# Two decoder layers on one core: both norm roots ahead of the first silu, one explicit silu table load a layer, the fourth mixer group's root from a pair of matmuls, and another list of order shifts

## The chip, the cores and the metric

The kernel runs on one core of a Trainium2 chip. The metric is the device time of one execution in microseconds (us), taken as the median of several runs. Before the change that is 2046.87 us (three runs, 2046.76 to 2048.48). One execution was also recorded by the hardware profiler; its own time is 2045.58 us, and the span from its first to its last instruction is 2043.8 us.

Five queues work side by side: PE (the matrix engine, TensorE), DVE (VectorE), ACT (ScalarE), POOL (GpSimd) and SP (SyncE, which here only issues DMAs). Each works through its own list in order. An instruction waits on semaphores for what other engines must have finished, and everything behind it in the same list waits with it.

## The reference

A decoder trunk of two layers on 1024 tokens of width 1024, in float32.

```python
for l in range(DEPTH):
    h = rmsnorm(x, attn_norm[l])
    proj = h @ w_in[l]
    ...
    y_a = mla_attention(...)          # latent attention, rotary key
    y_b = short_gated_conv(...)
    y_c = multiscale_pool(...)
    y_d = swa_sink_attention(...)     # sliding window, sinks
    groups = jnp.stack([y_a, y_b, y_c, y_d], axis=2)
    gf = gf * lax.rsqrt(jnp.mean(gf * gf, axis=-1, keepdims=True) + RMS_EPS)
    x = x + mixed @ w_o[l]
    h2 = rmsnorm(x, ffn_norm[l])
    gate, up = jnp.split(h2 @ w_gate_up[l], 2, axis=-1)
    x = x + (jax.nn.silu(gate) * up) @ w_down[l]
return rmsnorm(x, final_norm)
```

Each of the four mixer groups has its own RMSNorm (256 channels), and so has the input of the feed-forward part (1024 channels). "Root" below means the reciprocal square root of such a norm.

## The kernel before

**Layout.** Activations are held with channels on the 128 partitions and tokens along the free axis, in two halves of 512 tokens (`HALVES = (1, 0)`, so the second half of the tokens comes first). A float32 product is made of three matmuls of a reduced type (fp32r): each operand is split into a high part (`CAST` on ACT, L280) and a low remainder (`TENSOR_TENSOR` subtract on DVE, L283), and `mm3` (L260) adds high x high, high x low and low x high. Nearly all PE work is L260.

**A root.** `SumSq` squares the channel tiles on ACT (L324) and adds them on DVE (L326, L332). `rnorm` then sums over the partitions with a matmul against a matrix of ones and makes the root on ACT and DVE:

```python
if t in self.hl:                       # the sum was split into a pair
    for i, h in enumerate(self.hl.pop(t)):
        pe.matmul(p, ones_r, R.ap(h), start=i == 0, stop=i == 1)     # L340
else:
    pe.matmul(p, ones, a, start=True, stop=final is None)            # L343, plain float32
act.activation(r0, p, AF.Ln, scale=1.0 / n)                          # L349
act.activation(r0, r0, AF.Exp, scale=-0.5)                           # L350
act.activation(q, r0, AF.Square)                                     # L351
dve.scalar_tensor_tensor(...)                                        # L352, last reader of p
dve.scalar_tensor_tensor(...)                                        # L355
```

`SumSq(n, pair)` decides between the two forms: with `pair` the finished sum is split by ACT and DVE (`half_split`, one CAST and one subtract of 128x512) and the sum over partitions is two fp32r matmuls (L340). Without it the sum goes to PE as one float32 matmul, which the profile records as two (L343). `group_scale(g)` uses the pair for group b, and `norm_a` for group a; groups c and d use the float32 form. Each group has one root per token half and layer.

**The join of the two parts of a layer.** When the last group is ready, `out_last` finishes the output projection of one token half, adds it to the residual and splits the result for the feed-forward products. After the two halves come, in program order: the plain gate and up products of block f = 0 for the first half (`plain(0)`), that half's root, the silu of the gate (`plain_gates`: multiply by the root into a buffer of the ring "tp", then `silu`, which is ACT L1453 and a POOL multiply L1454), `combine(0)`, the product with up (`plain_acts`), the first products of blocks 1 and 2 (`early`), `combine(1)`, the second half's root, `plain(1)`, `combine(2)`, the second half's silu, `combine(3)`. `combine(j)` makes the sums and differences of the two halves that the seven-product scheme of the feed-forward part needs (ACT L1142, L1143; DVE L1132, L1145, L1151, L1153), each split into high and low. Its four results come from the ring "tp" too, which has three buffers.

**Tables.** ACT evaluates Ln and Exp with one loaded table and Silu with another. A load is an instruction of its own (`ACT_TABLE_LOAD`). One is written out at the start (L140, for Ln and Exp); the others are put in by the compiler in front of the function that needs them and carry that function's line.

**Order.** The program is traced once in Python order. Then a planner (class `Order`) lists each engine's instructions by estimated costs, PSUM banks are handed out from that plan, and a table of numbers, `MOVES`, shifts single instructions or short blocks in each engine's list: `e,i,n,d` takes n instructions at place i of engine e and puts them d places later (earlier if negative). The engines are numbered PE 0, ACT 1, DVE 2, POOL 3, SP 4. The final order is forced on the program; waits follow from the data, the buffers and the banks.

Of the kernel before, what the change touches and what calls it, by code (L numbers as in the profile page):

```python
# [18 lines left out]
P = 128  # L19
# [92 lines left out]
def trunk_kernel(ctx: ExitStack, tc: tile.TileContext, ins, out, given=None):  # L112
# [185 lines left out]
    class SumSq:  # L298
# [35 lines left out]
        def rnorm(self, t, cols=whole, tag="t", final=None):  # L334
# [15 lines left out]
            act.activation(r0, r0, AF.Exp, scale=-0.5)  # L350
# [67 lines left out]
    for l in range(L):  # L418
# [254 lines left out]
        def group_scale(g):  # L673

            sg = SumSq(2 * P, g in "b")
            for t in range(2):
                for c in range(2):
                    sg.add(t, F.ap(y[g][c][t]))
                r = sg.rnorm(t)
                for c in range(2):  # L680
                    a = F.ap(y[g][c][t])
                    mul_to(a, a, F.ap(r))
                F.free(r)
# [747 lines left out]
        def plain_gates():  # L1431
            for f, u, pg, pu in waiting:
                gate = tmp("tp")
                mul_to(gate, pg, r2[u])
                silu(gate, r2[u])
                gates.append((f, u, gate, pu))
            waiting.clear()

        def plain_acts():
            for f, u, gate, pu in gates:  # L1440
                acts[f][u] = F.half()
                mul_to(F.ap(acts[f][u]), pu, gate)
            gates.clear()
# [7 lines left out]
        def silu(g, r):  # L1451
            nonlocal last_silu
            last_silu = act.activation(g, g, AF.Silu)  # L1453
            pool.tensor_tensor(out=g, in0=g, in1=r, op=ALU.mult)  # L1454
# [123 lines left out]
        plain_acts()  # L1578
# [4 lines left out]
        r2.append(F.ap(ss2.rnorm(HALVES[1], tag="pv")))  # L1583
        plain(1)
# [692 lines left out]
```

## Time and profile before

| what | value |
|---|---|
| median of three runs | 2046.87 us (2046.76 to 2048.48) |
| the profiled execution | 2045.58 us, span 2043.8 us |
| mean granted PE clock | 0.998 of full speed |
| DMA moved | 302.37 MB, mean 148 GB/s |
| table loads on ACT | 11, of which 5 in each layer and 1 at the start |

How to read it: the page gives busy time per engine and the chain of work that ended last. Two more views are used. The list of waits names, for an engine, who released it and how long it sat idle. The timeline lists instructions in order of time, equal neighbours merged: start, length of the merged stretch, engine, line, operation, tiles, count, and in brackets the idle time just before it and what ended it. Matmuls overlap at their ends, so the distance between starts says more than the lengths. Layer 0 runs from the start to about 1004 us and layer 1 from there; the joins described above lie at 371 to 440 us and 1380 to 1445 us.

### The profile page before, as it was taken

How to read it: one execution, taken by the hardware profiler on the slowest of the kernel's cores; microseconds unless marked ns; L12 is line 12 of the kernel's file. 1: busy time of each engine (PE TensorE's matmuls, PEld its weight loads, DVE VectorE, ACT ScalarE, POOL GpSimd, SP SyncE). 2: the span in 40 equal slices, each digit the busy share in tenths (PEclk: the TensorE clock that was granted, in tenths of full speed). 3: DMA queues.
4: the chain of work that ended last, by engine and by line, in shares of the span. 5: the costliest groups of instructions: out<-in, count | busy, mean ns of one | idle time of the engine just before them, and what ended most of it. 6: DMA issues, size and time to landing. Idle time of an engine off the chain costs nothing.

```text
span 2043.8 us, 26551 instructions
## 1 busy us (share of the span) xinstructions
PE 2025.6 (99%) x9422; PEld 1677.5 (82%) x9422; DVE 1511.1 (74%) x2443; ACT 994.4 (49%) x1743; POOL 551.7 (27%) x420
## 2 busy tenths in 40 slices
PE   9999999999999999999999999999999999999998
PEld 7887888878888888888888888888788888888887
DVE  8789979987666578555657898899876666675555
ACT  7447657753333335444433676668433333354342
POOL 0100000037777772000002000000578667710000
PEclk9999999999999999999999999999999999999999
DMA  5211223335555557766413112242455555487642
GB/s 180 99 67 43 79 84 103 133 125 189 171 186 169 181 183 241 267 208 211 144 45 118 37 42 92 63 150 95 148 183 178 185 173 172 159 304 245 205 165 96
DMA packets 142119, 302.37 MB, mean 148 GB/s; under 512 B 13857, under 2 KB 60961, under 8 KB 141985
## 3 DMA queue, kind: packets, MB, share of 16 engines
q1 hardware_dynamic: 141984, 300.66, 43.9%
q8 instruction: 74, 1.21, 0.2%
q14 instruction: 61, 0.49, 0.1%
HBM read 212.00 MB, written 87.56 MB: 147 GB/s over the span
## 4 chain that ended last, share of the span: by engine, by line
PE 94%; DVE 3%; ACT 1%; issue 1%; DMA 0%; POOL 0%; SPq 0%; DVEq 0%; ACTq 0%
PE ps_mm L260 37%; PE ps_s L260 29%; PE ps_t L260 11%; PE ps_pv L260 8%; PE ps_pv L1044 2%; PE ps_t L1032 1%; PE ps_s L978 1%; PE ps_s L980 1%; PE ps_s L979 1%; PE ps_s L573 1%; PE ps_s L850 1%; PE ps_pv L634 1%; PE ps_t L622 1%; PE ps_t L343 1%; DVE u L286 0%
## 5 line engine op out<-in xcount | busy, mean ns | idle before, releaser
L260 PE MATMUL ps_mm<-u,u 128*128 128x512 f32 (+1 forms) x3378 | 833.3, 391 | 5.2 <-ACT u L280 4.0
L260 PEld LDWEIGHTS ps_mm<-u,u 128*128 128x128 f32 x3378 | 616.8, 188 | 131.6 <-ACT u L280 4.8
L260 PE MATMUL ps_s<-u,u 128*128 128x512 f32 x2670 | 634.4, 389 | 1.6 <-DVE tn L352 1.0
L260 PEld LDWEIGHTS ps_s<-u,u 128*128 128x128 f32 x2670 | 500.6, 188 | 108.2 <-DVE tn L352 1.5
L283 DVE TENSOR_TENSOR u<-u,u 128x1024 fp32r<-128x1024 f32 (+2 forms) x400 | 448.2, 1141 | 175.9 <-ACT u L280 137.8
L280 ACT CAST u<-u 128x1024 fp32r<-128x1024 f32 (+2 forms) x400 | 344.9, 881 | 395.4 <-PE ps_s L260 62.7
L260 PE MATMUL ps_t<-u,u 128*128 128x512 f32 (+1 forms) x1124 | 254.6, 377 | 0.4 <-DVE tn L352 0.4
L260 PEld LDWEIGHTS ps_t<-u,u 128*128 128x128 f32 x1124 | 202.3, 188 | 40.3 <-DVE tn L352 0.8
L1454 POOL TENSOR_TENSOR tp<-tp,u 128x512 f32<-128x512 f32 x80 | 127.6, 1595 | 342.2 <-ACT tp L1453 342.2
L260 PE MATMUL ps_pv<-u,u 128*128 128x512 f32 x744 | 177.4, 389 | 0.0
L260 PEld LDWEIGHTS ps_pv<-u,u 128*128 128x128 f32 x744 | 139.6, 188 | 29.0
L1453 ACT ACTIVATE tp<-tp 128x512 f32<-128x512 f32 x80 | 50.6, 633 | 214.5 <-DVE tp L359 214.3
L1041 POOL MEMSET u<- 128x128 f32 x32 | 6.2, 221 | 467.8 <-PE ps_mm L260 117.1
L749 POOL TENSOR_TENSOR u<-u,u 128x512 f32<-128x512 f32 x4 | 5.4, 1342 | 382.0 <-PE ps_t L622 289.9
L280 ACT CAST u<-ps_t 128x512 fp32r<-128x512 f32 (+3 forms) x132 | 65.2, 503 | 49.9 <-PE ps_t L1032 25.6
L285 ACT ACTIVATE u<-u,par 128x512 fp32r<-128x512 f32 x100 | 70.4, 717 | 28.0 <-DVE u L359 11.3
L283 DVE TENSOR_TENSOR u<-ps_t,u 128x512 fp32r<-128x512 f32 (+3 forms) x132 | 75.9, 580 | 10.6 <-ACT u L280 9.5
L1243 POOL TENSOR_TENSOR u<-u 128x512 f32<-128x512 f32 x38 | 73.3, 1930 | 27.9 <-DVE u L283 27.9
L1532 POOL TENSOR_TENSOR u<-u,u 128x352 f32<-128x352 f32 x64 | 75.9, 1185 | 7.6 <-DMA u<-in_w_dn 4.7
L1532 POOL TENSOR_TENSOR u<-u 128x352 f32<-128x352 f32 x64 | 75.2, 1175 | 8.9 <-DMA u<-in_w_dn 7.9
L286 DVE SCALAR_TENSOR_TENSOR u<-u,par,u 128x512 fp32r<-128x512 f32 x100 | 73.2, 744 | 5.5 <-ACT u L285 5.4
L359 DVE TENSOR_TENSOR tp<-tp,u 128x512 f32<-128x512 f32 x76 | 74.2, 976 | 1.5
(208 smaller groups left out, 2331.3 us busy)
## 6 DMA issues: line engine op xcount, KB each, us to landing
u<-in_w_gu SPq DMA_DIRECT2D x92, 512.0 KB, 3.9
ad<-u SPq DMA_DIRECT2D x154, 256.0 KB, 2.3
u<-ad SPq DMA_DIRECT2D x70, 512.0 KB, 5.0
u<-in_w_dn SPq DMA_DIRECT2D x64, 352.0 KB, 3.5
qd<-u SPq DMA_DIRECT2D x64, 352.0 KB, 2.5
u<-qd SPq DMA_DIRECT2D x32, 512.0 KB, 5.2
u<-in_w_in SPq DMA_DIRECT2D x28, 512.0 KB, 3.5
u<-in_w_dn SPq DMA_DIRECT2D x24, 512.0 KB, 5.4
```

The source lines that it names most:

```text
L260: pe.matmul(o, w, r, start=start and k == 0 and i == 0, stop=stop and k == n - 1 and i == 2, skip_group_check=again,)
L280: a = act.copy(hi, f)
L283: dve.tensor_tensor(out=lo, in0=f, in1=rd(hi), op=ALU.subtract)
L285: a = act.activation(hi, f, AF.Copy, scale=gain)
L286: dve.scalar_tensor_tensor(out=lo, in0=f, scalar=gain, in1=rd(hi), op0=ALU.mult, op1=ALU.subtract)
L343: pe.matmul(p, ones, a, start=True, stop=final is None)
L359: dve.tensor_tensor(out=o, in0=a, in1=b, op=ALU.mult)
L1044: pe.matmul(py[:, c0:], v_of(j, h), R.ap(s)[:, c0:], start=j == 0 and n == 0, stop=j == nj - 1 and n == 1,)
L1243: pool.tensor_tensor(out=q4, in0=q4, in1=F.ap(self.raw[1] + 1), op=ALU.add)
L1453: last_silu = act.activation(g, g, AF.Silu)
L1454: pool.tensor_tensor(out=g, in0=g, in1=r, op=ALU.mult)
L1532: pool.tensor_tensor(out=o, in0=a, in1=b, op=ALU.add)
```

## The change

**The fourth group.** `group_scale` now uses the pair form for groups b and d. Group d's two roots a layer change from one float32 matmul each to two fp32r matmuls each, and each gets one CAST on ACT and one subtract on DVE in front of it.

**Roots before silu.** `plain_gates` no longer calls `silu`; it only multiplies the gate by its root, into a half slot instead of a "tp" buffer. `plain_acts` now does the silu, the POOL multiply and the product with up, all in place in that slot. The first `plain_acts` call stands behind the second root, and between the two stands an explicit load of the silu table, ordered behind the second root's Exp (`behind(gate_table, ss2.exp)`); every silu is ordered behind that load.

**Order.** The planner first drops dependencies that follow from others (`shortest`), and `MOVES` is another list: 589 shifts instead of 476, of which 295 on DVE (223), 104 on ACT (96), 125 on SP (103), 36 on POOL (29) and 29 on PE (25).

```diff
-            act.activation(r0, r0, AF.Exp, scale=-0.5)
+            self.exp = act.activation(r0, r0, AF.Exp, scale=-0.5)
...
-            sg = SumSq(2 * P, g in "b")
+            sg = SumSq(2 * P, g in "bd")
...
         def plain_gates():
             for f, u, pg, pu in waiting:
-                gate = tmp("tp")
-                mul_to(gate, pg, r2[u])
-                silu(gate, r2[u])
-                gates.append((f, u, gate, pu))
+                s = F.half()
+                mul_to(F.ap(s), pg, r2[u])
+                gates.append((f, u, s, pu))
             waiting.clear()
 
         def plain_acts():
-            for f, u, gate, pu in gates:
-                acts[f][u] = F.half()
-                mul_to(F.ap(acts[f][u]), pu, gate)
+            for f, u, s, pu in gates:
+                silu(F.ap(s), r2[u])
+                mul_to(F.ap(s), pu, F.ap(s))
+                acts[f][u] = s
             gates.clear()
...
             last_silu = act.activation(g, g, AF.Silu)
+            behind(last_silu, gate_table)
             pool.tensor_tensor(out=g, in0=g, in1=r, op=ALU.mult)
...
         plain_gates()
         combine(0)
-        plain_acts()
         for w in early:
             w.split2()
         early[0].start()
         combine(1)
         r2.append(F.ap(ss2.rnorm(HALVES[1], tag="pv")))
+        gate_table = act.preload_act_table_set("silu_and_others")
+        behind(gate_table, ss2.exp)
+        plain_acts()
         plain(1)
...
 MOVES = (
-    "4,31,1,3 4,32,1,2 4,30,1,3 4,13,1,-2 4,12,1,-6 2,155,1,1 2,107,1,-1 2,159,1,12 4,40,1,3 "
+    "4,12,1,1 2,152,1,19 2,154,1,1 2,158,1,3 2,107,1,-1 1,102,1,3 2,154,1,2 4,36,1,1 "
...
-        self.need = [list(d.items()) for d in need]
-        self.feeds = [[] for _ in traced]
-        for k, d in enumerate(self.need):
+        self.need = self.shortest([list(d.items()) for d in need])
+        self.feeds = self.turned(self.need)
+
+    @classmethod
+    def shortest(cls, need):
+        feeds, left = cls.turned(need), [len(d) for d in need]
+        row = [k for k, d in enumerate(need) if not d]
...
+        for k in row:
+            b = e = 0
+            for p, sync in sorted(need[k], key=lambda x: -at[x[0]]):
+                if (e if sync else b) >> p & 1:
+                    continue
+                kept[k].append((p, sync))
...
```

In the program as a whole PE gets four matmuls more (9396 instead of 9392 instructions, a float32 matmul counted once), ACT four casts more and six table loads fewer, DVE four subtracts more. POOL and SP have as many instructions as before (384 tensor operations, 858 DMAs), in another order.

What the change does to the order is shown at three places. The first is ACT in layer 0 at the second half's root. `ps_pv` is the root's sum over partitions, "tn" its scratch, "tp" and "te" tiles are those of `combine`, and numbered u tiles are half or whole slots. Before:

```order
L349 ACT_TABLE_LOAD
L349 ACTIVATE tn<-ps_pv 128x512
L280 CAST u_4218<-tp 128x512
L350 ACT_TABLE_LOAD
L350 ACTIVATE tn<-tn 128x512
L280 CAST u_4215<-tp 128x512
L280 CAST u_4222<-tp 128x512
L1142 ACTIVATE te<-u_2542,par 128x512
L351 ACTIVATE tn<-tn 128x512
L1143 ACTIVATE te<-u_2312,par 128x512
```

And the same place now (u_4147 holds the first half's gate):

```order
L349 ACTIVATE tn<-ps_pv 128x512
L350 ACTIVATE tn<-tn 128x512
L280 CAST u_4169<-tp 128x512
L1584 ACT_TABLE_LOAD
L280 CAST u_4223<-tp 128x512
L1453 ACTIVATE u_4147<-u_4147 128x512
L280 CAST u_4220<-tp 128x512
L351 ACTIVATE tn<-tn 128x512
L1142 ACTIVATE te<-u_2550,par 128x512
L280 CAST u_4227<-tp 128x512
```

The two loads in front of Ln and Exp are gone, and behind Exp stand the explicit silu load and the first half's silu, both ahead of the root's Square (L351).

The second place is ACT a little later in layer 0, at the casts of the two 128x1024 operands that PE takes up next (u_4403 and u_4424 before, u_4411 and u_4432 now; they are the third weight blocks, `split3`, of f = 1 and f = 2). Before:

```order
L280 CAST u_4340<-tp 128x512
L1143 ACTIVATE te<-u_2086,par 128x512
L280 CAST u_4403<-u_4401 128x1024
L1453 ACT_TABLE_LOAD
L1453 ACTIVATE tp<-tp 128x512
L280 CAST u_4424<-u_4422 128x1024
L280 CAST u_4360<-tp 128x512
```

And now:

```order
L1143 ACTIVATE te<-u_2094,par 128x512
L1321 COPY tn<-ps_s 128x512
L280 CAST u_4349<-tp 128x512
L280 CAST u_4411<-u_4409 128x1024
L280 CAST u_4432<-u_4430 128x1024
L280 CAST u_2221<-tp 128x512
```

The second half's silu and its table load no longer stand between the two casts; that silu is now 14 rows behind them.

The third place is PE in layer 0 at the first root of group d (u_1935 is its sum before, u_1940 the pair now; "ones" is float32, "ones_r" fp32r). Before:

```order
L260 MATMUL ps_mm<-u_364,u_1837 128x512 x2
L343 MATMUL ps_t<-u_1935,ones 128x512
L260 MATMUL ps_mm<-u_364,u_1838 128x512
L260 MATMUL ps_mm<-u_376,u_1837 128x512 x2
L260 MATMUL ps_mm<-u_376,u_1838 128x512
```

And now:

```order
L260 MATMUL ps_s<-u_1783,vlo 128x512
L260 MATMUL ps_mm<-u_156,u_1929 128x512
L340 MATMUL ps_t<-u_1940,ones_r 128x512
L260 MATMUL ps_s<-u_1469,vhi 128x512
L340 MATMUL ps_t<-u_1940,ones_r 128x512
L260 MATMUL ps_s<-u_1469,vhi 128x512
```

One float32 matmul has become two fp32r ones, and they stand later, among the products that came after the root before.

More of the change, by code (lines that the diff above doesn't have):

```diff
@@ L1906, in __init__, with turned @@
                         need[k][p] = True
-        self.need = [list(d.items()) for d in need]
-        self.feeds = [[] for _ in traced]
-        for k, d in enumerate(self.need):
-            for p, sync in d:
-                self.feeds[p].append((k, sync))
+        self.need = self.shortest([list(d.items()) for d in need])
+        self.feeds = self.turned(self.need)
+    @staticmethod
+    def turned(need):
+        feeds = [[] for _ in need]
+        for k, d in enumerate(need):
+            for p, sync in d:
+                feeds[p].append((k, sync))
+        return feeds
+    @classmethod
[3 more added lines that the diff above has]
+        for k in row:
+            for j, _ in feeds[k]:
+                left[j] -= 1
+                if not left[j]:
+                    row.append(j)
+        at = {k: x for x, k in enumerate(row)}
+        before, ended, kept = [0] * len(need), [0] * len(need), [[] for _ in need]
+        for k in row:
+            b = e = 0
[3 more added lines that the diff above has]
+                kept[k].append((p, sync))
+                b |= before[p] | 1 << p
+                e |= ended[p] | (1 << p if sync else 0)
+            before[k], ended[k] = b, e
+        return kept
     @staticmethod
```

133 rows, old and new, of the table MOVES are left out of this document.

## The prediction

> **What bounds the kernel now.** I read the page first, then PE's list of waits, then the timeline of PE and ACT where the longest waits lie.
>
> ```profile
> PE 2025.6 (99%) x9422; PEld 1677.5 (82%) x9422; DVE 1511.1 (74%) x2443; ACT 994.4 (49%) x1743; POOL 551.7 (27%) x420
> PE 94%; DVE 3%; ACT 1%; issue 1%; DMA 0%; POOL 0%; SPq 0%; DVEq 0%; ACTq 0%
> ```
>
> PE is busy 2025.6 of 2043.8 us and carries 94% of the chain that ended last. So time can only come from matmuls that go, from PE's few idle stretches, or from a slower PE clock. PE's list of waits is short:
>
> ```profile
> PE ps_mm L260 <- ACT u L280: 4.0, 2, 2.0
> PE ps_s L260 <- DVE tn L352: 1.0, 1, 1.0
> PE ps_s L347 <- ACT tn L346: 0.6, 1, 0.6
> PE ps_t L260 <- DVE tn L352: 0.4, 1, 0.4
> ```
>
> The first, second and fourth row are four waits, and all lie in the joins of the two layers. Here is PE in layer 0, with one row of steady work from the chain ahead of it, 24 matmuls in 5.44 us, or 0.227 us each:
>
> ```profile
> 437.13 5.44 PE ps_mm L260 x24
> ...
> 407.79 4.24 PE L260 MATMUL ps_s<-u,u 128*128 128x512 f32 x18
> 413.07 3.03 PE L260 MATMUL ps_s<-u,u 128*128 128x512 f32 x12 [1.04 <-DVE tn L352]
> ...
> 422.37 0.61 PE L260 MATMUL ps_mm<-u,u 128*128 128x512 f32 x2
> 424.96 2.57 PE L260 MATMUL ps_mm<-u,u 128*128 128x512 f32 x10 [1.98 <-ACT u L280]
> 427.36 0.39 PE L260 MATMUL ps_s<-u,u 128*128 128x512 f32 x1
> ```
>
> From 407.79 the 18 matmuls take until 411.88, and the next starts at 413.07: 1.19 us lost (the bracket says 1.04, since ends overlap). From 422.37 two matmuls last until 422.82, and the next starts at 424.96: 2.14 us. Layer 1 has the same pair:
>
> ```profile
> 1415.56 0.84 PE L260 MATMUL ps_pv<-u,u 128*128 128x512 f32 x3
> 1416.79 3.69 PE L260 MATMUL ps_t<-u,u 128*128 128x512 f32 x15 [0.39 <-DVE tn L352]
> ...
> 1431.20 0.61 PE L260 MATMUL ps_mm<-u,u 128*128 128x512 f32 x2
> 1433.82 4.14 PE L260 MATMUL ps_mm<-u,u 128*128 128x512 f32 x10 [2.01 <-ACT u L280]
> 1437.80 0.40 PE L260 MATMUL ps_s<-u,u 128*128 128x512 f32 x1
> ...
> 1434.10:1437.60 3.50, 3.50 (x10) 2.67 (x10) 3.35 (x6) 0.71 (x2) 0.08 (x1) 0.51 0.20 75
> ```
>
> They cost 0.55 us (1416.24 to 1416.79) and 2.17 us (1431.65 to 1433.82). After the second, ten matmuls take 3.98 us from start to start where layer 0 needs 2.40. The window in the last row shows why: the granted clock is 0.51 there. That is another 1.58 us.
>
> **What the change removes: the waits.** ACT in layer 0, with the one DVE row:
>
> ```profile
> 405.77 1.28 ACT L349 ACT_TABLE_LOAD   x1
> 407.06 0.60 ACT L349 ACTIVATE tn<-ps_pv 128x512 f32<-128x512 f32 x1
> 407.56 0.61 ACT L280 CAST u<-tp 128x512 fp32r<-128x512 f32 x1
> 408.19 1.28 ACT L350 ACT_TABLE_LOAD   x1
> 409.48 0.63 ACT L350 ACTIVATE tn<-tn 128x512 f32<-128x512 f32 x1
> ...
> 411.68 0.61 ACT L351 ACTIVATE tn<-tn 128x512 f32<-128x512 f32 x1
> 412.32 0.69 DVE L352 SCALAR_TENSOR_TENSOR tn<-ps_pv,tn 128x512 f32<-128x512 f32 x1 [0.46 <-ACT tn L351]
> ...
> 419.13 0.57 ACT L1321 COPY tn<-ps_s 128x512 f32<-128x512 f32 x1
> ...
> 420.99 1.04 ACT L280 CAST u<-u 128x1024 fp32r<-128x1024 f32 x1
> 422.05 1.28 ACT L1453 ACT_TABLE_LOAD   x1
> 423.34 0.63 ACT L1453 ACTIVATE tp<-tp 128x512 f32<-128x512 f32 x1
> 423.88 1.03 ACT L280 CAST u<-u 128x1024 fp32r<-128x1024 f32 x1
> ```
>
> *First wait of a layer.* The second root must reload the tables for Ln and again for Exp, 2 x 1.28 us, because the first half's silu ran in between. PE's next tile takes over the bank that L352 frees last; in layer 0 33 matmuls stand between them, 7.5 us, which is less than the root needs. In the order of the change no reload stands there. One load and one silu come ahead of the Square instead (1.28 + 0.63), so the root itself gets only 2 x 1.28 - 1.91 = 0.65 us shorter. What decides is the place: in the built program the root's bank is next taken after 84 matmuls (19 us), in layer 1 after 59 (13.4 us) instead of 24. DVE's L352 stands late in its list too, 28 and 20 rows behind the first root's, but by DVE's steps (below) still some 3 and 2 us ahead of that use. I take both waits as gone: **-1.19 and -0.55 us**.
>
> *Second wait.* PE needs the second 128x1024 cast, and ahead of it on ACT stand the table load and the silu, 1.91 us, which now come elsewhere (second place of the order). What is late next? ACT's copy of PE's product (L1321, the 419.13 row) starts a chain: 0.57 + 0.61 + 1.04 + 1.03 = 3.25 us until the second cast ends, some 0.4 us after the product. PE has 21 matmuls ahead of its use, 4.8 us, so 1.1 us are to spare; in layer 1, with one cast more, 33 matmuls are 7.5 us against 4.3. DVE's steps:
>
> ```profile
> 414.33 0.60 DVE u L283
> ...
> 419.15 0.67 DVE tp L1153
> ...
> 422.20 1.21 DVE L283 TENSOR_TENSOR u<-u,u 128x1024 fp32r<-128x1024 f32 x1
> 423.33 0.68 DVE L1132 SCALAR_TENSOR_TENSOR tp<-tp,te 128x512 f32<-128x512 f32 x1
> ```
>
> In layer 0, 37 operations of DVE lie between the root and the low part of that operand: 3 of 128x1024 at 1.13 us from start to start, 8 with a gain at 0.67 and 26 at 0.60, 24.4 us, against 109 matmuls, 24.7 us. So DVE comes next, and its reserve is what it starts ahead of the root: 23 matmuls (5.2 us) after the first root PE does the second, while DVE goes on as soon as the first root has passed ACT, some 3.1 us (0.60 + 0.63 + 0.61 + 0.61 and the way through PE), 2 us ahead. I take the wait as gone: **-2.14 and -2.17 us**. If half of DVE's reserve is missing, 1 us a layer comes back.
>
> *The slow clock* follows layer 1's wait, and I let it go with the wait: **-1.58 us**. The Trainium skill, "TensorE: Matmul & The Clock Gate", section "What's actually happening", has the clock fall to half only after an idle window of about 3.4 us. Here 2.0 us of idle time sufficed in layer 1 and not in layer 0; by that rule the slow stretch would have another cause and stay, which is a rival below.
>
> The rest of the silu edit I cost at nothing: silu, POOL product and multiply are as many as before, off PE's chain, and the slot held earlier instead of a "tp" buffer gives `combine` its ring back. Its cover is the distance to PE's next use of the gate's bank. By the 1.28 rows six loads fewer free 7.7 us of ACT, nearly all beside PE. The Trainium skill, "ScalarE: Activation LUTs", section "What ACT_TABLE_LOAD costs", adds a drain of 1380 ns to each switch. The trace does not show it: the load at 422.05 starts 0.02 us after the cast before it ends, and the silu starts 0.01 us after the load; by the page ACT would gain 16 us (an estimate: 6 x 2.66), still beside PE, and the sum would be the same.
>
> **What it adds: the pair for group d.**
>
> ```profile
> 189.34 1.02 PE L343 MATMUL ps_t<-u,ones 128*128 128x512 f32 x2
> 189.80 1.26 PE L260 MATMUL ps_mm<-u,u 128*128 128x512 f32 x3
> ...
> 391.59 0.62 PE L340 MATMUL ps_pv<-u,ones_r 128*128 128x512 f32 x2
> 392.05 0.86 PE L260 MATMUL ps_s<-u,u 128*128 128x512 f32 x3
> ...
> 172.00:212.00 40.00, 40.00 (x172) 31.35 (x171) 38.44 (x65) 29.34 (x54) 0.00 (x0) 1.00 0.17 50
> ```
>
> Both forms take 0.46 us to the next start, but the three matmuls behind the float32 root take 1.26 us and those behind the pair 0.86. A pair is 0.40 us cheaper on PE; four of them: **-1.60 us**. It adds a cast (0.61) and a subtract (0.60) ahead of each root. In the window around group d, DVE is busy 38.44 of 40 us, so 1.2 us more a layer just fits; if it doesn't, PE waits up to 1.2 us in each layer and most of the 1.6 is gone. PE's order has the second root 25 matmuls (5.7 us) behind the first, against some 5.3 us of root, add and split. I take nothing for it and keep 0 to +2.4.
>
> **The list.** 589 shifts move work in all stretches. SP and POOL issue the same instructions, and DMA and POOL have 0% of the chain. Elsewhere the trace leaves at most the L347 wait of 0.6 us and single hundreds of nanoseconds to win, some 2 us in all; a loss has no bound in any row. I take 0, the value nearest to PE's 99%.
>
> **Sum.** -1.19 - 0.55 - 2.14 - 2.17 - 1.58 - 1.60 = -9.23 us. On the profiled execution (span 2043.8, its time 2045.58, 1.8 outside the span) that is 2036.35; the median of the runs is 1.29 above that execution, and on it the sum gives **2037.6**.
>
> **Rivals.**
> - *The new wait is DVE's.* With the tables out of the way PE reaches the joins 3.3 us earlier, and DVE (24.4 us of work for 24.7 us of matmuls) is short by 1 to 2 us a layer, around the joins or at group d. For it: 38.44 of 40 us. Against: in the joins DVE itself idled for ACT's loads (0.46 us in the row above). It gives back 2 to 4.5 us: 2040 to 2042.
> - *The slow clock stays.* If it hangs on the stretch and not on the wait, 1.58 comes back: 2039.2.
> - *The list closes more* than the named waits: 2035.6 at the 2 us above.
> - *The list opens as much as the change closes*, though no load or silu stands where it stood: 2043 to 2049, no difference.
> - *Slower.* DVE's list has 295 shifts, and where PE has no reserve, each operation put one step too early ahead of the one PE waits for costs 0.60 us. PE hides little in the attention stretch, where it hangs on DVE's softmax. To be 0.2% slower it takes 9.2 + 4.1 = 13.3 us, 22 such places of 295; at 23 or more the time is above 2051. Against it: before, the same kind of list leaves no PE wait there over 0.6 us.
>
> **How the numbers follow.** Forecast 0.58; DVE's wait 0.15; slow clock stays 0.08; list closes more 0.05; no difference 0.08; slower 0.06. About 0.2% (4.1 us) is what a measurement of this kernel can tell from no change. The first four are faster by more: 0.86; no difference 0.08; slower 0.06. The range 2034.5 to 2042.0 leaves out the last two and little else.
>
> **What would show it.** PE's waits on L280 and on L352 in the joins gone, with no entry above 1 us but the start; ACT with five loads; granted clock 1.00 right through layer 1's join; 20 instead of 28 L343 records of 512 columns, and eight more of L340. A new PE wait on DVE L283 in the joins or near group d shows the first rival. The prediction is wrong if PE's busy time falls by less than 1 us, or if waits of the same length appear under other names.

## The result, and the profile after

The changed kernel takes 2036.06 us (median of six runs, 2035.82 to 2036.47), the kernel before 2047.48 us (six runs, 2046.76 to 2048.48): a ratio of 0.9945, with a 95% interval of 0.9932 to 0.9957. The two profiled executions are nearer to each other: 2036.14 against 2045.58 us, 9.44 us less, where the medians differ by 11.4.

The page of the changed kernel (busy time of the engines, then the shares of the chain that ended last), then PE's list of waits (us in total, times, longest):

```profile
PE 2023.0 (99%) x9422; PEld 1676.2 (82%) x9422; DVE 1509.5 (74%) x2447; ACT 987.5 (49%) x1741; POOL 540.7 (27%) x420
PE 97%; DVE 2%; ACT 0%; DMA 0%; issue 0%; DVEq 0%; ACTq 0%
```

```profile
PE ps_pv L476 <- DVE ones L134: 1.1, 1, 1.1
PE ps_s L347 <- ACT tn L346: 0.6, 1, 0.6
PE ps_mm L260 <- DVE te L359: 0.2, 1, 0.2
PE ps_pv L1044 <- DVE u L283: 0.2, 1, 0.2
```

The four waits of the joins are gone; what is left above 0.2 us lies at the start (L476) and at the very end (L347), where it was before. PE's share of the chain rose from 94 to 97%. ACT in layer 0's join now reads so (timeline; the last row is the second half's silu):

```profile
403.18 0.57 ACT L349 ACTIVATE tn<-ps_pv 128x512 f32<-128x512 f32 x1
403.79 0.63 ACT L350 ACTIVATE tn<-tn 128x512 f32<-128x512 f32 x1
...
404.94 1.28 ACT L1584 ACT_TABLE_LOAD   x1
...
406.76 0.63 ACT L1453 ACTIVATE u<-u 128x512 f32<-128x512 f32 x1
...
417.31 0.56 ACT L1321 COPY tn<-ps_s 128x512 f32<-128x512 f32 x1
417.77 0.62 ACT L280 CAST u<-tp 128x512 fp32r<-128x512 f32 x1
418.30 2.01 ACT L280 CAST u<-u 128x1024 fp32r<-128x1024 f32 x2
420.20 1.14 ACT L280 CAST u<-tp 128x512 fp32r<-128x512 f32 x2
...
425.91 0.64 ACT L1453 ACTIVATE u<-u 128x512 f32<-128x512 f32 x1 [1.24 <-DVE u L359]
```

Ln and Exp follow each other without a reload, the one table load stands at 404.94, 13 us ahead of the two 128x1024 casts, these run back to back, and the second half's silu comes 5.6 us behind them, without a load. The windows of the two joins (columns: window, length, busy time of PE, PEld, DVE, ACT and POOL with counts, granted clock, DMA share, GB/s):

```profile
402.00:437.00 35.00, 35.00 (x156) 28.48 (x155) 33.70 (x48) 24.16 (x39) 9.78 (x7) 1.00 0.23 76
1402.00:1442.00 40.00, 40.00 (x178) 32.84 (x177) 37.62 (x53) 26.85 (x43) 8.30 (x6) 1.00 0.20 66
```

PE is busy throughout at full clock, beside a DVE that is 96 and 94% full.

Where the 9.44 us went, by stage: for every matmul I took the distance to the next start, less what that shape takes in steady work, and added these excesses up.

| stage | before | after |
|---|---|---|
| layer 0, group d (170 to 210 us) | 0.69 | 1.04 |
| layer 0, attention (210 to 370) | 3.66 | 4.37 |
| layer 0, join (370 to 450) | 4.55 | 0.79 |
| layer 1, group d (1180 to 1215) | 0.41 | 0.62 |
| layer 1, attention (1215 to 1375) | 3.86 | 3.57 |
| layer 1, join (1375 to 1455) | 4.79 | 0.49 |

The joins give 8.06 us (3.76 and 4.30), the half clock of layer 1 among them. The cheaper form of the four roots gives 1.6 beside this table (4 x 0.40, its steady cost), of which 0.56 come back around group d. The rest is small and of both signs; the largest piece is 0.4 us behind PE's last matmul (9.63 us from its start to the end of the span before, 9.21 now). Attention of layer 0 varied from 3.66 to 4.33 us between three profiles of the kernel before, so 0.7 us there means nothing.

### The profile page after: what moved, and what is told of

It reads as the page before. It is cut to its first block, busy times and chain, and to the rows that moved or that the text cites. A ratio compares the mean times of both kernels' runs of the same rounds, so it can differ in the third digit from the quotient of the medians.

```text
span 2034.4 us, 26578 instructions
## 1 busy us (share of the span) xinstructions
PE 2023.0 (99%) x9422; PEld 1676.2 (82%) x9422; DVE 1509.5 (74%) x2447; ACT 987.5 (49%) x1741; POOL 540.7 (27%) x420
## 3 DMA queue, kind: packets, MB, share of 16 engines
q8 instruction: 74, 1.21, 0.3%
## 4 chain that ended last, share of the span: by engine, by line
PE 97%; DVE 2%; ACT 0%; DMA 0%; issue 0%; DVEq 0%; ACTq 0%
PE ps_mm L260 37%; PE ps_s L260 30%; PE ps_t L260 12%; PE ps_pv L260 8%; PE ps_pv L1044 2%; PE ps_t L1032 1%; PE ps_s L978 1%; PE ps_s L980 1%; PE ps_s L979 1%; PE ps_s L573 1%; PE ps_s L850 1%; PE ps_pv L634 1%; PE ps_t L622 1%; DVE u L283 0%; PE ps_t L343 0%; PE ps_t L340 0%
## 5 line engine op out<-in xcount | busy, mean ns | idle before, releaser
L283 DVE TENSOR_TENSOR u<-u,u 128x1024 fp32r<-128x1024 f32 (+2 forms) x404 | 442.2, 1115 | 180.2 <-ACT u L280 143.5
L1455 POOL TENSOR_TENSOR tp<-tp,u 128x512 f32<-128x512 f32 x76 | 120.6, 1587 | 188.3 <-ACT tp L1453 182.6
L1243 POOL TENSOR_TENSOR u<-u 128x512 f32<-128x512 f32 x38 | 69.2, 1821 | 31.2 <-DVE u L283 31.2
L359 DVE TENSOR_TENSOR tp<-tp,u 128x512 f32<-128x512 f32 x76 | 75.8, 997 | 1.4
L324 ACT ACTIVATE tn<-u 128x512 f32<-128x512 f32 (+1 forms) x91 | 52.6, 596 | 49.8 <-DVE u L1726 45.8
```

Of the source, the lines that this page charges most:

```text
L283: dve.tensor_tensor(out=lo, in0=f, in1=rd(hi), op=ALU.subtract)
L324: act.activation(q, f, AF.Square)
L359: dve.tensor_tensor(out=o, in0=a, in1=b, op=ALU.mult)
L1243: pool.tensor_tensor(out=q4, in0=q4, in1=F.ap(self.raw[1] + 1), op=ALU.add)
```

## The experiments

Each of these kernels keeps the planner's order and the list of shifts of the kernel it starts from; instructions are added, dropped or shifted in the finished lists, so that nothing else moves. Times in us; the ratio is to the kernel before on the same chip, with its 95% interval.

| run | profiled execution | median | ratio |
|---|---|---|---|
| before, again | 2045.65 | 2046.90 | 1.0004 (0.9995 to 1.0014) |
| before, silu behind the second cast | 2044.99 | 2044.95 | 0.9996 (0.9986 to 1.0005) |
| before, one load for the second root | 2042.05 | 2042.66 | 0.9983 (0.9973 to 0.9992) |
| both of these | 2041.51 | 2042.26 | 0.9979 (0.9970 to 0.9988) |
| both, DVE's multiply two places later | 2041.05 | 2042.09 | 0.9977 (0.9967 to 0.9986) |
| one load, gate in a half slot | 2051.54 | 2050.41 | 1.0016 (1.0007 to 1.0026) |
| the same, silu, multiply and store placed anew | 2041.36 | 2042.13 | 0.9976 (0.9966 to 0.9986) |
| after, again | 2036.33 | 2036.41 | 0.9950 (0.9936 to 0.9963) |
| after, group d in float32, no splits | 2037.04 | 2036.90 | 0.9952 (0.9940 to 0.9965) |
| after, group d in float32, splits kept | 2037.54 | 2037.47 | 0.9954 (0.9940 to 0.9968) |
| after, 3 and 5 more loads | 2048.93 | 2050.07 | 1.0015 (1.0006 to 1.0025) |
| before, a third time | 2046.46 | one run | |

### One load instead of two for the second root

```diff
+        act.preload_act_table_set("natural_log_exp_and_others")   # in ACT's list just ahead of the second Ln
         r2.append(F.ap(ss2.rnorm(HALVES[1], tag="pv")))
```

> The kernel before, with one explicit load of the table that holds both Ln and Exp in front of the second root's Ln, so that each layer's join has one reload for that root instead of two; the silu stays where it was. My theory: L352 comes 1.28 us earlier, the waits behind it (1.19 and 0.55 us) go, and since the chain of the second wait starts with PE's own product, that wait stays at 2.1 us: 1.74 us less than before. Rival: ACT is what runs late, so the second wait does not move and grows by what the first gives (3.3 and 2.7 us): no difference. If the wait in layer 1 then exceeds 2.0 us, the slow clock should be there as before.

The waits for L352 vanish in both layers, and PE's list of waits then begins with the second waits alone:

```profile
PE ps_mm L260 <- ACT u L280: 3.4, 2, 1.9
```

From start to start they cost 2.09 us in layer 0 (2.14 before) and 1.60 in layer 1 (2.17). There was no half clock before the end. Of the 3.53 us that the profile lost, 1.58 are the half clock and 1.95 the waits; my theory had 1.74. That is near for a mixed reason: layer 1's second wait, which the theory left as it was, shrank by 0.57 us, and small losses elsewhere took that back. The rival (the second wait grows by what the first gives) is out. So the reloads held the first wait, and one explicit load in place of two is already enough to end it, in the old order and with the silu where it was.

### The second half's silu behind the second cast

```diff
 L280 CAST u<-u 128x1024
-L1453 ACT_TABLE_LOAD
-L1453 ACTIVATE tp<-tp 128x512
 L280 CAST u<-u 128x1024
+L1453 ACT_TABLE_LOAD
+L1453 ACTIVATE tp<-tp 128x512
```

> The kernel before, with the second half's first silu and its table load issued behind the second 128x1024 cast instead of between the two, in both layers; nothing else. My theory: the cast comes 1.91 us earlier (1.28 + 0.63), so the waits of 2.14 and 2.17 us shrink to 0.2 to 0.3 us each (-3.8 us), and the slow clock goes with layer 1's wait (-1.58 us): 5.4 us less than before, a profile of about 2040.2 us. Rival A (the slow clock hangs on the stretch): 3.8 us less, and a clock of 0.5 still at about 1432 us. Rival B (another chain was nearly as late): a wait of 1 us or more comes back under another name, and less than 2.5 us are won. The first waits of the joins (L352) stay at 1.19 and 0.55 us in all cases.

> The kernel before with both edits: one load for the second root, and the second half's silu behind the second 128x1024 cast. My theory: the parts add, -1.74 - 3.8 - 1.58 = -7.1 us, a profile of about 2038.5 us, no wait above 0.4 us in the joins, no slow clock. What then remains to the changed kernel (2036.14) is 2.3 us, of which 1.6 the four roots and 0.5 the rest of the second waits. Rival (the list of shifts and the earlier roots carry the gain): less than 4 us of the 9.4.

The cast came earlier as meant, and PE no longer waited for it. But the profile fell by 0.6 us only, less than the half clock that was gone with the old wait. Rival B is right. PE's list of waits of the first of the two runs, then one row of its PE and its DVE in layer 0:

```profile
PE ps_mm L260 <- DVE u L283: 1.2, 1, 1.2
...
PE ps_s L260 <- DVE u L283: 0.9, 1, 0.9
```

```profile
428.17 0.49 PE L260 MATMUL ps_mm<-u,u 128*128 128x512 f32 x1 [1.16 <-DVE u L283]
...
423.83 0.69 DVE L1132 SCALAR_TENSOR_TENSOR tp<-tp,te 128x512 f32<-128x512 f32 x1
426.83 0.69 DVE L359 TENSOR_TENSOR u<-ps_s,tp 128x512 f32<-128x512 f32 x1 [2.31 <-POOL tp L1454]
427.44 1.28 DVE L283 TENSOR_TENSOR u<-tp,u 128x512 fp32r<-128x512 f32 x2
428.64 0.69 DVE L1151 TENSOR_TENSOR tp<-te 128x512 f32<-128x512 f32 x1
429.24 0.75 DVE L1153 SCALAR_TENSOR_TENSOR tp<-u,nffn,tp 128x512 f32<-128x512 f32 x1
430.02 1.23 DVE L283 TENSOR_TENSOR u<-u,u 128x1024 fp32r<-128x1024 f32 x1
```

Load and silu feed POOL's product (L1454), and that feeds DVE's multiply with up (L359 at 426.83), for which all of DVE stands still for 2.31 us. Behind it in DVE's list wait the two subtracts that PE needs at 428.17. So the load held PE by ACT's list and by DVE's list at once, the second hardly shorter than the first. The kernel with both edits has the same wait (1.17 and 0.93 us) and gives 4.1 us where 7.1 were expected, just above the bound of its rival (less than 4). In the joins themselves the second edit adds nothing: PE's excess there, counted as in the table by stage, is 5.7 us with both edits and 5.5 with one load alone.

### The multiply two places later

```diff
-L359 TENSOR_TENSOR u<-ps_s,tp 128x512
 L283 TENSOR_TENSOR u<-tp,u 128x512
 L283 TENSOR_TENSOR u<-tp,u 128x512
+L359 TENSOR_TENSOR u<-ps_s,tp 128x512
 L1151 TENSOR_TENSOR tp<-te 128x512
```

> The kernel before with one load for the second root, the second half's silu behind the second 128x1024 cast, and now also DVE's multiply of the gate with up (it waits for the POOL product behind that silu) two places later, behind the two subtracts that it held up. New theory for the second wait: load and silu held PE on two ways at once, by the cast on ACT and by POOL's product and this multiply in DVE's list. Then PE's waits for L283 (1.17 and 0.93 us, with 0.4 us around each) go or fall below 0.4 us, and the kernel is 2 to 3 us below the one without this edit (its profile was 2041.5), at 2038.5 to 2039.5. Rival: the third subtract (128x1024), which must stay behind the multiply because of the buffers, takes the wait over, and less than 1 us is won.

The wait at 1433 fell from 1.1 to 0.33 us and that at 424 from 1.38 to 0.6, but new ones of 0.23 and 0.72 us came behind them, and 0.46 us were won: the rival. By the program's buffers, which no run tests, the multiply can't go further back: L1151 writes the buffer of the three-buffer ring "tp" that the multiply must read first; L1153 follows L1151; and the subtract of 128x1024 overwrites the slot that L1153 still reads.

### The gate in a half slot, in the old order

This is the part of the change that breaks the ring, put into the kernel with one load: the second half's gate goes into a half slot and is worked on in place. The lines apply to the second half alone; in the finished lists the silu and the multiply move too, as the expectation says.

```diff
-                gate = tmp("tp")
+                acts[f][u] = F.half()
+                gate = F.ap(acts[f][u])
...
-                acts[f][u] = F.half()
                 mul_to(F.ap(acts[f][u]), pu, gate)
```

> The kernel before with one load for the second root (as in the run with that edit alone), and with the second half's gate in a half slot instead of a buffer of the ring tp, worked on in place there; so its silu can stand behind the casts of combine's third result and the multiply with up behind the fourth subtract, which the ring of three buffers forbade. The first half's silu stays ahead of the second root, the float32 roots and the old list of shifts stay. New theory for the second wait: what held PE was the whole path of load, silu, POOL product and multiply, which the ring tied to combine's later results, and the 128x1024 subtract behind them. Then the stalls of 2.1 us in each join go without any new wait above 0.4 us, no half clock, and against the run with one load (profile 2042.05) 2.8 + 1.5 = 4.3 us go: a profile of 2037.5 to 2038.2, with runs within 1 us of each other. Rival: the roots ahead of the silu and the new list carry it; then less than 2 us go, and a wait of 1 us comes back under another name.

The stalls of 2.1 us went, as the theory says, and still the kernel became 9.5 us slower than with one load alone. PE and ACT of layer 0, then SP, whose rows are DMA issues:

```profile
437.68 2.81 PE L260 MATMUL ps_mm<-u,u 128*128 128x512 f32 x7 [2.89 <-ACT u L280]
...
437.01 0.62 ACT L280 CAST u<-u 128x512 fp32r<-128x512 f32 x1 [5.80 <-DMA u<-gd]
...
432.03 0.32 SPq L1621 DMA_DIRECT2D ad<-u  x1
432.44 0.88 SPq L1248 DMA_DIRECT2D u<-gd  x2
```

The multiply, now later, is stored by SP (L1621 here, L1614 in the kernel before), and that store stands in SP's list ahead of two loads. They went out at 432.44 instead of 428.24 in the kernel before (427.54 with one load), and PE waited 2.89 us for their data. Layer 1 has the same wait, and each of the two was followed by a half clock. Two further waits of 1.07 and 0.93 us, for DVE's L1451, follow in layer 0.

```diff
-L1614 DMA ad<-u 128x512
 L1248 DMA u<-gd 128x512
 L1248 DMA u<-gd 128x512
+L1614 DMA ad<-u 128x512
```

> As the run before it on the gate in a half slot (kernel before, one load for the second root, second half's gate worked on in place in a half slot), but with the silu directly behind the casts of combine's first two results, where ACT idled for 2.1 us, the multiply with up right behind the second 128x1024 subtract, and SP's store of that product behind the two loads from gd instead of ahead of them. In the run before, that store waited for the later multiply, and the loads behind it in SP's list, whose data PE waited 2.9 us for, came 4.2 us late. Theory: with that third way (multiply, store, loads, cast) opened too, the stalls of 2.1 us in the joins are gone and no wait above 0.5 us takes their place, no half clock: a profile of 2037.3 to 2038.5, 3.5 to 4.8 us below the run with one load alone (2042.05), within 2 us of the changed kernel; what remains is the 0.5 to 0.7 us of the roots and the list. Rival: the slack is in the whole order, so that only another list finds it: a wait of 1 us or more appears elsewhere, and the profile stays above 2040.

With that third way opened the waits of 2.1 and 2.9 us are gone. In the joins remain 1.04 us behind 445.87 in layer 0 and 0.74 us behind 1435.67 in layer 1. PE and DVE of layer 0, then DVE and POOL of layer 1:

```profile
447.13 2.99 PE L260 MATMUL ps_pv<-u,u 128*128 128x512 f32 x12 [0.87 <-DVE u L1451]
446.31 0.68 DVE L1451 SCALAR_TENSOR_TENSOR u<-ps_s,u 128x512 f32<-128x512 f32 x1
...
1434.38 2.20 DVE L283 TENSOR_TENSOR u<-u,u 128x1024 fp32r<-128x1024 f32 x1
1433.77 1.72 POOL L1458 TENSOR_TENSOR u<-u,u 128x512 f32<-128x512 f32 x1 [21.17 <-ACT u L1457]
```

In layer 0 PE waits for L1451, the negated product (`neg_mul`) of a later block, not for the gate that was moved. That operation comes at 446.31, where the run with one load alone has it at 445.88 (L1447 there): DVE came no earlier, and PE's earlier stall had hidden that. In layer 1 PE waits for the 128x1024 subtract. It took 2.20 us beside POOL's product of the moved gate (L1458); in the kernel before, 161 such subtracts with POOL idle took 1.21 to 1.23 us each.

The profile is 0.7 us below the run with one load alone, not 3.5, and above 2040 with a new wait of 1 us: what the rival said. By stages the joins gave 1.4 us (5.5 to 4.1), and attention of layer 0, which the edit does not touch, took 0.9 of it back. So the path from the gate held PE at the stalls of 2.1 us, but freed by hand in the old order it brings PE only as far as the next late operation. The changed kernel's store stands behind those two loads too, and PE waits nowhere in its joins, with 1.3 us of excess left there. The 2.8 us between 4.1 and 1.3 go with the rest of the change (the roots ahead of the first silu, the new order); no run separates these.

### The roots of group d

```diff
-                for i, h in enumerate(self.hl.pop(t)):
-                    pe.matmul(p, ones_r, R.ap(h), start=i == 0, stop=i == 1)
+                pe.matmul(p, ones, a, start=True, stop=True)     # group d only, in the same place
```

> The changed kernel once more, as the measure for the two runs with float32 roots on the same chip. Expected: a profile within 0.5 us of 2036.14, timed runs within 1 us of one another, no stretch of half clock before the end, since no window of PE has 2 us of idle time.

> The changed kernel with group d's four roots as one float32 matmul each, as before, and without the cast and the subtract in front of them; all else stands where it stood. My theory (a pair is 0.40 us cheaper on PE, less what its cast and subtract cost PE): 1.6 us more than the changed kernel, less the 0.35 and 0.21 us that the changed kernel loses around group d, so +1.0 to +1.6 us. Rival (DVE is full there, 38.4 of 40 us, and the pair costs as much as it saves): no difference, within 0.4 us, or less than the changed kernel.

> The changed kernel with group d's four roots as one float32 matmul each, but with the cast and the subtract still made (their result is not used). My theory: the matmul alone, +1.6 us and all of PE's small waits near group d as in the changed kernel. What this run has above the one without the splits is the price of the splits: 0 to 0.6 us by my theory, 1.2 us or more (two subtracts of 0.60 us a layer) by the rival that DVE is full there.

Without pair and splits the kernel is 0.5 us (medians) to 0.7 us (profiles) slower, less than the 1.0 to 1.6 of my theory and more than the rival's nothing. With the splits kept it is 1.1 to 1.2 us slower. The matmul's own price is as predicted: from a root's start to the sixth next, 1.79 us in float32 against 1.38 as a pair, 0.41 each. But around group d PE's small waits are 0.86 us shorter with the float32 form (0.50 and 0.49 us of excess, against 1.24 and 0.61): about half of what the pair saves (0.67 instead of 0.86 against the first profile of the changed kernel). With the splits kept they are as short, 0.6 and 0.5 us, though my theory for that run had them as in the changed kernel. So it is not the cast and the subtract that bring these small waits, but the faster root: PE is then presumably ahead of its data, which no run shows. The splits' 0.5 us lies within what two profiles of one kernel differ by, so I put no cause to it.

### How much reserve the second cast has

```diff
 L280 CAST u<-u 128x1024
+L1587 ACT_TABLE_LOAD x3          (x5 in layer 1)
 L280 CAST u<-u 128x1024
```

> The changed kernel with more table loads on ACT between the two 128x1024 casts of each join, three in layer 0 (3.84 us) and five in layer 1 (6.40 us); the order of all else is the same. It measures the reserve that the prediction gave the second cast (1.1 us in layer 0, 3.2 us in layer 1): by it PE waits 2.7 us in layer 0 and 3.2 us in layer 1, +5.9 us. Rival: the later casts and DVE's subtracts behind them are late too, and the reserve is 0: up to 3.8 and 6.4 us, +10.2. The slow clock: by the two profiles with half clock, PE idle for over 2.1 us of one window of 3.413 us (the grid in which all clock stretches are measured) gives 3.41 us of half clock behind it (+1.6 us each), and up to 1.9 us of idle time does not. So with waits of 2.7 and 3.2 us at least one stretch of half clock is likely in a run, and timed runs differ by 1.6 us and more. The rule that a full window of 3.4 us must be idle would give none in layer 0.

PE stalled for 3.92 us in layer 0 and 5.58 in layer 1 (start to start, less the steady distance), for 3.84 and 6.40 us of loads. So the reserve is nothing in layer 0 and 0.8 us in layer 1: the rival. PE in both layers, then ACT in layer 0:

```profile
424.85 1.22 PE L260 MATMUL ps_s<-u,u 128*128 128x512 f32 x2 [3.76 <-ACT u L280]
1437.05 0.80 PE L260 MATMUL ps_s<-u,u 128*128 128x512 f32 x1 [5.41 <-ACT u L280]
...
419.36 3.86 ACT L1587 ACT_TABLE_LOAD   x3
423.23 1.04 ACT L280 CAST u<-u 128x1024 fp32r<-128x1024 f32 x1
424.18 1.13 ACT L280 CAST u<-tp 128x512 fp32r<-128x512 f32 x2
```

PE did not wait for the 128x1024 cast, done at 424.27, but for the first 128x512 cast behind it, done at 424.80, and so in layer 1. In the changed kernel layer 0's cast ends at about 420.8 and PE takes it at 420.92.

### The slow clock

> The kernel before, once more, for the question why its profiled execution (2045.58 us) lies 1.2 to 2.9 us below all of its timed runs. Theory: the half-speed stretch of 3.4 us (cost 1.58 us) is set off by the 2-us waits for the second 128x1024 cast, by chance, in none, one or both layers; then this profile again shows a clock of 0.5 only right behind those waits, the number of such stretches may differ from one, and the span differs by about 1.6 us for each. Rival (the slow clock hangs on the stretch of the program): again exactly one, in layer 1 at about 1434 us, and the span is 2043.8 within 0.3 us.

> The kernel before a third time, for the clock alone. Theory: the clock is judged in a grid of windows of 3.413 us whose start lies anywhere from execution to execution; a window in which PE was busy under about 1.6 us (below 1.49 in all seven seen, above 1.81 in none) is followed by a window at half speed. So it depends on how the grid cuts the two stalls (422.8 to 425.0 and 1431.7 to 1433.8 us): where it cuts neither near its middle both are followed by half clock, or one or none, each worth 1.6 us. If the grid again starts at about 4.0 us behind the span's start, as in the two profiles so far: half clock in layer 1 alone, span 2043.8. If it starts at 5.5 to 6.5 us: in layer 0 (at about 426 us) and not in layer 1. Rival (the clock hangs on the stretch of the program): half clock in layer 1 alone, wherever the grid starts.

Both repeats showed one half clock before the end, in layer 1 as the rival had it, and spans of 2043.9 and 2044.7 us. What I had named for the third (layer 0, from where the grid started, 5.49 us) was wrong: the program had shifted along by 0.9 us. What decides shows in windows laid on the grid, in pairs of one window and the next: the kernel before (layer 1), its third run (layer 0, then 1), the run with one load (layer 0), and the run with more loads (layer 0).

```profile
1430.74:1434.15 3.41, 1.40 (x6) 0.86 (x5) 2.02 (x4) 3.23 (x4) 1.24 (x1) 1.00 0.38 142
1434.16:1437.56 3.40, 3.40 (x9) 2.62 (x8) 3.31 (x6) 0.65 (x2) 0.02 (x1) 0.50 0.20 77
```

```profile
421.92:425.32 3.40, 2.02 (x9) 1.31 (x7) 3.01 (x5) 3.37 (x5) 0.36 (x1) 1.00 0.01 1
425.33:428.73 3.40, 2.86 (x12) 2.36 (x13) 2.46 (x5) 1.54 (x3) 0.90 (x1) 1.00 0.64 229
...
1432.27:1435.67 3.40, 1.40 (x7) 0.84 (x6) 1.94 (x4) 3.39 (x5) 1.28 (x1) 1.00 0.28 112
1435.68:1439.08 3.40, 3.40 (x10) 2.60 (x9) 3.37 (x6) 0.05 (x1) 0.00 (x0) 0.50 0.20 77
```

```profile
422.64:426.05 3.41, 1.81 (x8) 1.50 (x9) 2.07 (x5) 2.59 (x4) 1.27 (x1) 1.00 0.47 154
426.06:429.46 3.40, 3.40 (x17) 2.66 (x16) 3.37 (x5) 1.69 (x4) 0.00 (x0) 1.00 0.42 125
```

```profile
421.07:424.48 3.41, 0.02 (x1) 0.00 (x0) 0.00 (x0) 3.39 (x4) 0.00 (x0) 1.00 0.43 154
424.49:427.89 3.40, 3.04 (x7) 2.46 (x8) 3.06 (x5) 1.33 (x3) 0.00 (x0) 0.50 0.00 0
```

Wherever PE was busy for 1.49 us or less of such a window (eight windows in five profiles) the next ran at half clock; at 1.81 us and more none did. (The expectation of the run with more loads had a half clock follow over 2.1 us of idle time and none up to 1.9; the windows give 1.9 and 1.6.) Behind PE's last work every profile ends at half clock, by the same border, and there it costs PE nothing. So the same stall of 2.1 us costs 1.6 us more when it falls inside one window (layer 1) and nothing more when a boundary cuts it (layer 0). It does not hang on the stretch of the program: two edits that shortened or shifted layer 1's stall had full clock there.

This also fits the medians. Of 77 runs of the kernel before that were timed beside the experiments, 37 had a mean granted clock of 0.998 and took 2045.74 us on average, 40 had 0.997 or 0.996 and took 2047.44: 1.7 us more, about one more half clock (3.41 us at half speed is 0.0008 of the mean). That is inferred from the averages: the three profiles of this kernel are all of the first kind, and none shows two half clocks ahead of its end. The changed kernel's ten timed runs lie within 1.3 us.

## Why the prediction was right, and where it was not

The prediction, 2037.6 us in a range of 2034.5 to 2042.0, holds: 2036.06 was measured. That its sum on the profile, 2036.35, lies within 0.2 us of the 2036.14 measured is partly luck: the roots gave about 1 us less than their term, the joins 0.4 us more, and places that it did not name the rest.

- **The first waits** (-1.19 and -0.55 us): right in size, and right that the reloads held them. The step said that "what decides is the place", since the root gets only 0.65 us shorter. One load less, 1.28 us, takes both waits away in the old place, so a later place is not needed; whether the changed kernel needs it was not tested.
- **The second waits** (-2.14 and -2.17 us): right in size, since the joins gave 8.06 us where 7.63 were summed up (3.33 and 4.30 by layer, half clock included). Right for a reason that was half of it. The step read "ahead of it on ACT stand the table load and the silu, 1.91 us, which now come elsewhere"; taking these from ahead of the cast alone leaves stalls of 1.4 and 1.1 us. The prediction had silu, POOL product and multiply "off PE's chain". It overlooked the way through POOL and DVE's multiply, which the ring "tp" tied to the subtracts behind it, and the way from that multiply through SP's store to the loads behind it. The change opens all of them, by the half slot and by its order; how the gain divides between the two was not measured.
- **The reserve** (1.1 and 3.2 us): wrong. It was counted for the second cast; the 128x512 cast right behind it is needed earlier and has 0 and 0.8 us. That cost nothing here, but by these rows the next 0.2 us that are put ahead of it in layer 0 would.
- **The slow clock** (-1.58 us): right to let it go with the wait. The rule of the Trainium skill ("TensorE: Matmul & The Clock Gate", section "What's actually happening") has windows of 3413 ns that run free of the kernel, and half clock after an idle window. The windows agree: stretches of 3.413 us or multiples of it, starting 4.0 to 7.2 us after the span did. An idle window is not needed: 1.9 us without a matmul out of 3.41 sufficed, 1.6 did not.
- **The roots** (-1.60 us): the term that was mis-sized. 0.5 to 0.7 us were measured. The price per root held (0.41 for 0.40), but about half of it turned into small waits of PE around group d, which the step put at nothing, with an upper bound of 2.4.
- **The list at 0**: not shown. Without a new order the freed gate path gave 0.7 us (1.4 in the joins), so a part of the waits' gain belongs to the order; and the 0.4 us behind PE's last matmul are shown by both profiles of the changed kernel and by none in the old order.
- **The step from the profile to the median** (+1.29 us) failed by 1.4 us (the changed kernel's median lies 0.08 below its profile): it was carried over from a kernel half of whose runs show about one half clock more than its profile, to one whose two profiles show none before the end.
- **The rivals**: no new wait of PE on DVE above 0.2 us came up, so the first is out for the joins of the changed kernel; in the old order with the gate freed it is what came next. What ate half of the roots' gain is not shown to be DVE: with DVE's splits kept and the float32 root the small waits stay short. The slow clock did not stay.

Open: what holds PE around group d, what the roots ahead of the first silu and the new order give each for itself, and whether the old order could be arranged as well by hand.

## What to carry to other kernels

A wait's releaser names the last of several ways. Before counting a wait as gone, follow everything that the moved instruction feeds (here POOL, a multiply, a ring of buffers, a store, the loads behind the store), and ask for each which list it blocks. A buffer ring shared by two chains ties their orders together, and here a slot of its own gave little (1.4 us in the joins) in an order made without it. Where kernels stall for about 2 us, compare profiles only together with their granted clock.

## What the runs showed of the hardware

- A stall of 2.1 us, far shorter than a clock window, costs 1.6 us more when one window holds all of it, and nothing when a boundary cuts it; the runs of the kernel before with a lower mean clock are 1.7 us longer on average.
- A table load that is followed by the load of another table on ACT takes its 1.28 us again each time (3 in 3.86 us), with no gap between them.
- DVE and POOL at work side by side can slow each other: 161 of DVE's 128x1024 subtracts in the kernel before took 1.21 to 1.23 us with POOL idle, and all longer ones, up to 2.34 us, ran beside it; POOL's product (L1454) took 1.27 to 1.31 us with DVE idle and up to 3.43 us beside it.
